# A prefix-conditioned diffusion block on one core: changes at its front, in the work beside the expert blocks, and in how the last two expert blocks reach the output

## The chip, the cores and the metric

The kernel runs on one core of a Trainium2 chip. The metric is the device time of one execution in microseconds (us); the time of the kernel before is the median of three runs. The profile comes from one further, profiled execution.

The engines are named as in the profile: PE (matrix products), PEld (its weight loads), DVE (vector), ACT (scalar functions), POOL (general), SP (only issues transfers). DMA is the core's 16 DMA engines. Each engine works through its own instructions in order and waits on semaphores of the others.

## The reference

512 latent tokens (x) and 256 context tokens (ctx), 1024 wide, all float32, one layer:

```python
sh1, sc1, g1, sh2, sc2, g2 = _modulation(c, w_mod, b_mod, 6)
hx = _rmsnorm(x, norm_mix_pre) * (1 + sc1) + sh1      # the same for ctx
# projections of hx and hc by w_in; a retention scan and a gated
# delta-rule scan, both in two directions, started from the context's state;
# gated merge, output projection
x = x + g1 * _rmsnorm(mixer_out, norm_mix_post)
h2 = _rmsnorm(x, norm_ffn_pre) * (1 + sc2) + sh2
x = x + g2 * _rmsnorm(_moe(h2), norm_ffn_post)
```

In `_moe` each token picks 8 of 64 experts. Each expert computes `(silu(xe @ w_gate) * (xe @ w_up)) @ w_down` (1024 to 256 to 1024) for its tokens in blocks of up to 128; the results, times the token's weight, are summed by token, and a shared expert is added.

## The kernel before

The work is written in stages, and a scheduler of the kernel's framework orders the instructions of each engine. The order below is that of the profiled execution.

- Front (0 to about 62 us). `w_mod` comes in as 16 pieces of 512 KB (tile `wm`, issued on SP at L300) that take turns in five buffers. Each piece is split into a high and a low part (`wmu`: ACT cast L100, DVE difference L107), because a float32 product is made as three products of such parts (L111 to L113). Then x and ctx are normalized (L286) and turned (L338).
- Delta-rule stage (to about 290 us). `w_in` comes in pieces (`raw`, L148), split into `wu`. The scan's triangular systems are built from `E`, `rk`, `br`, stored to DRAM arrays `cd` and `zd` to change their layout, and solved on DVE in 31 steps. `zd` is filled with zeros first (L382, issued on ACT). `bd` receives the turned betas (L527 to L534).
- Retention stage (290 to about 600 us), output projection, second norm and router (to about 700 us). None of it is changed.
- Expert stage (to about 1390 us). There is one block of 128 tokens for each of the 64 experts, and a 65th block for tokens that did not fit into an expert's first block. The token list of a first block (`slots`) comes from sorting; the ranks (L1311 to L1344) and the function `extra` (L1372) find the tokens of the further block. In step e of the loop (L1410) block e is projected (`proj`: 48 products, accumulated in `acc`), block e-1 is turned and projected down (`down`, products `cs<-wd,aT` at L1258), and the weights of later blocks are converted (`wh`, `wl`) and loaded (`w` and `wgu` in six buffers, `wd` in three). `down` scales its result into `y` and a transfer of POOL adds it to the rows of `acc0` or `acc1` in DRAM (L1263).
- Further blocks. A device loop (`For_i`, L1439) handles blocks beyond the 65th; its count `nx` is computed on the chip and is 0 for these inputs. All engines meet at this loop.
- End. `acc1` is loaded (L1456), added to `acc0` (L1458), squared and summed (L1461), normalized (L127 on POOL, L1464), added to x (L1468, or by adding transfers of POOL for two of the four row tiles, L1466) and stored.

## Time and profile before

| | us |
|---|---|
| median of 3 runs | 1429.2 (1427.99 to 1431.35) |
| the profiled execution | 1428.3 |
| its span | 1426.5 |
| PE busy | 1334.9 (94%) |
| DVE busy | 901.3 (63%) |
| ACT busy | 654.1 (46%) |
| POOL busy | 404.4 (28%) |

The span runs from the first to the last instruction of the profile. PE's busy share is a mean over all stages; what a change in a stage is worth depends on what is waited for in that stage. Half a granted clock (PEclk 0.50 for a stretch) means TensorE at 1.2 GHz instead of 2.4 GHz.

### The profile page before, as it was taken

The numbers are of one execution on the slowest core, as the hardware profiler recorded it, in microseconds if no ns is written. First come the engines' busy times: TensorE is split into PE (matmuls) and PEld (weight loads), VectorE is DVE, ScalarE is ACT, GpSimd is POOL, SyncE is SP. The second block draws the span as 40 slices with busy tenths as digits, with TensorE's granted clock in tenths as the row PEclk, the third lists the DMA queues.
The fourth block names the chain that finished last, engine by engine and source line by source line (L and its number), as shares of the span: only waits on it lengthen the run. The fifth ranks groups of instructions, "written<-read, shape, count | busy, mean of one in ns | idle before, by whom it ended". The sixth has DMA issues, their size and how long they took to land.

```text
span 1426.5 us, 20707 instructions
## 1 busy us (share of the span) xinstructions
PE 1334.9 (94%) x7848; PEld 1081.8 (76%) x7848; DVE 901.3 (63%) x1269; ACT 654.1 (46%) x926; POOL 404.4 (28%) x330
## 2 busy tenths in 40 slices
PE   6989888899999999999989999999999999999990
PEld 2658777898887777777878787888888787878770
DVE  5635696457676556547676666666666666666643
ACT  5634431553333222334445555565655555555531
POOL 0313644865320000012402222222222222223312
PEclk9899998999999999999999999999999999999995
DMA  8643521202326578575889999999999999999954
GB/s 291 187 111 104 132 59 27 59 16 80 81 56 181 173 218 233 149 244 198 302 305 339 355 367 342 369 348 354 363 361 358 362 371 350 367 355 360 314 182 126
DMA packets 138841, 340.51 MB, mean 239 GB/s; under 512 B 28218, under 2 KB 84574, under 8 KB 113780
## 3 DMA queue, kind: packets, MB, share of 16 engines
q1 hardware_dynamic: 110952, 289.46, 57.1%
q0 software_dynamic: 19584, 38.99, 10.8%
q10 hardware_dynamic: 8204, 10.72, 2.5%
q8 instruction: 63, 1.03, 0.3%
q14 instruction: 38, 0.31, 0.1%
HBM read 326.59 MB, written 48.31 MB: 263 GB/s over the span
## 4 chain that ended last, share of the span: by engine, by line
PE 46%; DMA 5%; DVE 1%; POOL 1%; issue 0%; ACT 0%; DVEq 0%; SPq 0%; POOLq 0%; ACTq 0%
PE cs L1258 15%; PE acc L112 8%; PE acc L111 8%; PE acc L113 8%; PE ci L1227 4%; DMA wd<-in_w_down_dram 2%; PE ci L1057 2%; DMA wgu<-in_w_up_dram 1%; PE acc L1247 1%; PE acc L1069 1%; DMA w<-acc 1%; POOL fr L127 0%; DMA acc<-y,sl_i 0%; DMA acc<-y,slots 0%; PE ci L1010 0%
## 5 line engine op out<-in xcount | busy, mean ns | idle before, releaser
L111 PE MATMUL acc<-wh,xT 128*128 128x256 f32 x1040 | 305.2, 293 | 0.0
L113 PE MATMUL acc<-wh,xT 128*128 128x256 f32 x1040 | 294.7, 283 | 0.0
L112 PE MATMUL acc<-wl,xT 128*128 128x256 f32 x1040 | 294.4, 283 | 0.0
L1164 DVE TENSOR_TENSOR wl<-w,wh 128x2048 fp32r<-128x2048 f32 x88 | 201.5, 2292 | 87.8 <-PE acc L112 87.7
L1263 POOL DMA_INDIRECT acc<-y,slots x64 | 101.9, 1592 | 479.8 <-ACT y L1260 430.2
L1258 PE MATMUL cs<-wd,aT 128*128 128x512 f32 x520 | 234.3, 593 | 3.3 <-DMA wd<-in_w_down_dram 2.2
L1162 ACT CAST wh<-w 128x2048 fp32r<-128x2048 f32 x88 | 167.2, 1902 | 94.4 <-PE acc L113 76.3
L111 PEld LDWEIGHTS acc<-wh,xT 128*128 128x128 f32 x1040 | 199.9, 192 | 0.2 <-issue 0.2
L112 PEld LDWEIGHTS acc<-wl,xT 128*128 128x128 f32 x1040 | 199.7, 192 | 0.2 <-issue 0.2
L113 PEld LDWEIGHTS acc<-wh,xT 128*128 128x128 f32 x1040 | 199.2, 191 | 0.0
L1258 PEld LDWEIGHTS cs<-wd,aT 128*128 128x128 f32 x520 | 93.9, 190 | 97.3 <-issue 94.7
L1230 DVE TENSOR_TENSOR xT<-ci,xT 128x512 fp32r<-128x512 f32 x130 | 89.3, 687 | 89.7 <-ACT xT L1229 86.2
L100 ACT CAST wu<-raw 128x1024 fp32r<-128x1024 f32 (+1 forms) x73 | 74.9, 1036 | 110.3 <-DMA raw<-in_w_in_dram 76.2
L1164 DVE TENSOR_TENSOR wl<-wgu,wh 128x2048 fp32r<-128x2048 f32 x42 | 96.3, 2292 | 42.7 <-PE acc L112 41.5
L111 PE MATMUL acc<-hTx,wu 128*128 128x512 f32 (+1 forms) x296 | 119.3, 403 | 1.8 <-ACT wu L100 1.8
L113 PE MATMUL acc<-hTx,wu 128*128 128x512 f32 (+1 forms) x296 | 118.3, 400 | 1.6 <-DVE wu L107 1.6
L112 PE MATMUL acc<-hLx,wu 128*128 128x512 f32 (+1 forms) x296 | 117.9, 398 | 0.0
L107 DVE TENSOR_TENSOR wu<-raw,wu 128x1024 fp32r<-128x1024 f32 (+1 forms) x61 | 77.5, 1277 | 62.8 <-ACT wu L100 62.8
L1162 ACT CAST wh<-wgu 128x2048 fp32r<-128x2048 f32 x42 | 79.7, 1898 | 53.8 <-PE acc L113 36.5
L1227 PEld LDWEIGHTS ci<-ident,xg 128*128 128x128 f32 x520 | 73.6, 192 | 29.9 <-issue 29.5
L1219 POOL DMA_INDIRECT xg<-h2d,slots x64 | 71.5, 1117 | 35.6 <-issue 18.3
L1227 PE MATMUL ci<-ident,xg 128*128 128x128 f32 x520 | 80.4, 279 | 0.0
(492 smaller groups left out, 2362.4 us busy)
## 6 DMA issues: line engine op xcount, KB each, us to landing
wd<-in_w_down_dram SPq DMA_DIRECT2D x64, 1024.0 KB
w<-in_w_gate_dram SPq DMA_DIRECT2D x43, 1024.0 KB
w<-in_w_up_dram SPq DMA_DIRECT2D x43, 1024.0 KB
raw<-in_w_in_dram SPq DMA_DIRECT2D x56, 512.0 KB
wgu<-in_w_gate_dram SPq DMA_DIRECT2D x21, 1024.0 KB
wgu<-in_w_up_dram SPq DMA_DIRECT2D x21, 1024.0 KB
mraw<-in_w_mod_dram SPq DMA_DIRECT2D x32, 512.0 KB
wm<-in_w_mod_dram SPq DMA_DIRECT2D x16, 512.0 KB
```

The lines of the kernel that those rows point to most:

```text
L100: nc.scalar.copy(dst, src)
L107: (self.nc.gpsimd if eng == "pool" else self.nc.vector).tensor_tensor(dst, src, hi.bitcast(F32), op=OP.subtract)
L111: mm(out, ah, bh, start=start, stop=False)
L112: mm(out, ah, bl, start=False, stop=False)
L113: mm(out, al, bh, start=False, stop=stop)
L1162: nc.scalar.copy(h[:, i:i + max(n, 1024)], w[:, i:i + max(n, 1024)])
L1164: eng(l[:, i:i + n], w[:, i:i + n], h[:, i:i + n].bitcast(F32), op=OP.subtract)
L1219: nc.gpsimd.indirect_dma_start(xg[:, :], None, self.h2d[:, :], bass.IndirectOffsetOnAxis(ap=ix, axis=0), bounds_check=511, oob_is_err=False)
L1227: nc.tensor.transpose(ps[:, k * 128:k * 128 + 128], xv[:, :, c * 4 + k], self.ident)
L1230: tt(l, ps, h.bitcast(F32), op=OP.subtract)
L1258: nc.tensor.matmul(ps, aT[:, m], wd[:, s], start=k == 0, stop=k == 1)
L1263: nc.gpsimd.indirect_dma_start(self.accd[acc][:, :], bass.IndirectOffsetOnAxis(ap=sx, axis=0), y[:, :], None, bounds_check=511, oob_is_err ...
```

## The change

1. The `wm` pieces 3 to 10 go to eight slices of the storage that later holds `hTx` and `hLx`, so there are eleven buffers instead of five.
2. The zeros for `zd` are written in rows of 774 elements instead of 258, out of `gcv`, and the transfer is issued on ACT behind the copy of `gT`.
3. The turned betas (`bd`) are made behind the first two `prep` calls, and the first q projection ahead of the loop over `vtok`.
4. Ranks, the columns of the further block and its list are made in steps 3, 5 and 7 of the expert loop instead of ahead of it.
5. Blocks 63 and 64 are no longer added to DRAM. Their results are split in two parts (`yhl`, `down_parts`) and a one-hot matrix (`places`) times each part puts the rows in place, in eight PSUM banks; `acc0 + acc1` is added to that. x is loaded for all four row tiles, and all stores are plain ones.
6. The loop over further blocks stands behind the stores, and would do the end again after each block.

```diff
+        wms = [t[:, i] for t in [self.hxpool.tile([128, 4, 1024], F32, name="wm", tag=tag) for tag in ("b0", "b1")] for i in range(4)]
...
-                w = (self.rawp if i % 5 < 3 else wp).tile([128, 1024], F32, name="wm", tag="raw")
+                w = wms[i - 3] if 3 <= i < 11 else self.rawp.tile([128, 1024], F32, name="wm", tag="raw")
...
-        zero = gp.tile([128, 258], F32, name="zero", tag="E")
+        zero = gcv[:, 2:4].rearrange("p a n -> p (a n)")[:, 0:774]
         nc.gpsimd.memset(zero, 0.0)
-        nc.scalar.dma_start(zd.rearrange("t h n -> (t h n)").rearrange("(p a n) -> p a n", p=128, n=258), zero[:, None, :].to_broadcast([128, 12, 258]))
...
-        nc.scalar.copy(gT[:, 0:512], px[0:16])
+        with tc.issue_after(nc.scalar.copy(gT[:, 0:512], px[0:16]).ins):
+            nc.scalar.dma_start(zd.rearrange("t h n -> (t h n)").rearrange("(p a n) -> p a n", p=128, n=774), zero[:, None, :].to_broadcast([128, 4, 774]))
...
-        for t in range(6):
+        prep(0)
+        prep(1)
+        for dr in range(2):
+            ps = self.pc()
+            brd = gc.tile([128, 6, 4], F32, name="brd", bufs=2)
...
+            nc.sync.dma_start(bd[dr], bt)
+        for t in range(2, 6):
             prep(t)
...
+        q0 = conv_in(0, False)
         for t in range(6):
             pk = self.pc()
...
+        def down_parts(aT, ws, wd):
+            y = T8("yhl")
+            for c in range(2):
+                ps = self.pc()
...
+                h, l = y[:, c * 512:c * 512 + 512], y[:, 1024 + c * 512:1536 + c * 512]
+                nc.scalar.activation(h, ps, AF.Copy, scale=ws)
+                nc.vector.scalar_tensor_tensor(l, ps, ws, h.bitcast(F32), op0=OP.mult, op1=OP.subtract)
+            return y
...
+        def places(oh, row):
+            at = q.tile([128, 4], F32, name="at", bufs=2)
+            for t in range(4):
+                ts(at[:, t:t + 1], row, -128.0 * t, None, op0=OP.add)
+                ts(oh[:, t], cst("r0"), at[:, t:t + 1], None, op0=OP.is_equal)
...
+            def place(t, j):
+                oh, y = blocks[j]
+                for c in range(2):
...
+                    for i in range(2):
+                        nc.tensor.matmul(PS[t, c], oh[:, t], y[:, i * 1024 + c * 512:i * 1024 + c * 512 + 512],
+                                         start=j == 0 and i == 0, stop=j == len(blocks) - 1 and i == 1)
+
+            def out(t, s, eng):
+                nc.vector.scalar_tensor_tensor(mg[t][:, s], mg[t][:, s], r[:, t:t + 1], x1[t][:, s], op0=OP.mult, op1=OP.add)
+                eng.dma_start(self.out[t * 128:t * 128 + 128, s], mg[t][:, s])
...
+            for t in range(4):
+                for c in range(2):
+                    s = slice(c * 512, c * 512 + 512)
+                    tt(m[t][:, s], PS[t, c], m[t][:, s], op=OP.add)
...
+                nc.scalar.activation(junk, m[t], AF.Square, scale=D ** -0.5, accum_out=r[:, t:t + 1])
+                nc.scalar.activation(r[:, t:t + 1], r[:, t:t + 1], AF.Identity, bias=self.eps)
+                if t % 2 == 0:
+                    tt(mg[t], m[t], g2p, op=OP.mult)
+                    nc.gpsimd.tensor_tensor(r[:, t:t + 1], r[:, t:t + 1], self.mhalf, op=OP.pow)
+                else:
+                    nc.gpsimd.tensor_tensor(mg[t], m[t], g2p, op=OP.mult)
+                    nc.gpsimd.tensor_tensor(r[:, t:t + 1], r[:, t:t + 1], self.mhalf, op=OP.pow)
+                if t:
+                    out(t - 1, slice(0, 1024), nc.scalar if t % 2 else nc.sync)
+            out(3, slice(0, 512), nc.scalar)
+            out(3, slice(512, 1024), nc.sync)
...
-        self.xtra = extra()
         for e in range(NE + 2):
...
+            if e == 3:
+                ranks()
+            if e == 5:
+                xcols = extra_cols()
+            if e == 7:
+                self.xtra = extra_list(*xcols)
...
-            if e > 0:
-                down(aT, SL[e - 1], W[e - 1], raw(e - 1, 2), 1 if e - 1 > NE - 4 else (e - 1) % 2)
+            if e > NE - 1:
+                Y.append(down_parts(aT, W[e - 1], raw(e - 1, 2)))
+            elif e > 0:
+                down(aT, SL[e - 1], W[e - 1], raw(e - 1, 2), (e - 1) % 2)
...
+            if e == NE - 1:
+                m1, x1 = halves(NE - 2), halves(NE - 1)
...
+            if e == NE:
+                m = halves(NE)
+                for t in range(4):
+                    nc.sync.dma_start(m[t], self.accd[0][t * 128:t * 128 + 128])
+                for t in range(4):
+                    tt(m[t], m[t], m1[t], op=OP.add)
+
+        finish(m, x1, list(zip(OH, Y)))
```

Three places show how the order moves. The first is ACT in the delta-rule stage, where `wu<-raw` converts pieces of `w_in`, `rcA` and `rcB` are copies of products that wait for those, and `gT` is a later one. Before:

```order
L100 CAST wu_620<-raw_618 128x1024
L382 DMA zd_497<-zero_500 1536x1x258
L415 COPY rcA_595<-acc_525 128x512
L415 COPY rcA_597<-acc_526 128x512
L100 CAST wu_637<-raw_635 128x1024
L100 CAST wu_654<-raw_652 128x1024
L100 CAST wu_715<-raw_713 128x128
L415 COPY rcB_669<-acc_599 128x512
L415 COPY rcB_671<-acc_600 128x512
L434 COPY gT_768<-acc_718 16x512
```

Now:

```order
L100 CAST wu_614<-raw_612 128x1024
L417 COPY rcA_589<-acc_519 128x512
L417 COPY rcA_591<-acc_520 128x512
L100 CAST wu_631<-raw_629 128x1024
L100 CAST wu_648<-raw_646 128x1024
L100 CAST wu_709<-raw_707 128x128
L100 CAST wu_820<-raw_818 128x1024
L417 COPY rcB_663<-acc_593 128x512
L417 COPY rcB_665<-acc_594 128x512
L100 CAST wu_885<-raw_883 128x1024
L436 COPY gT_762<-acc_712 16x512
L437 DMA zd_493<-gcv_481 512x1x774
```

The store of the zeros has moved from between the pieces that feed `rcA` and `rcB` to behind `gT`, with a third of the rows.

The second is PE at the start of the expert loop, around the down projection of block 0 (`cs<-wd,aT`); `ci<-colx,oh` are the products of the further block's list, `ci<-ident,xg` turns gathered tokens, `acc<-...,xT` projects a block. Before:

```order
L113 MATMUL acc_5976<-wh_5922,xT_5784 128x256
...
L1258 MATMUL cs_6056<-wd_5609,aT_6009 128x512 x2
L1370 LDWEIGHTS oh_5877
L1370 MATMUL ci_5876<-colx_5866,oh_5877 128x6
L1370 LDWEIGHTS oh_5880
L1370 MATMUL ci_5876<-colx_5866,oh_5880 128x6
L1227 MATMUL ci_5959<-ident_61,xg_5691 128x128
L1370 LDWEIGHTS oh_5883
L1370 MATMUL ci_5876<-colx_5866,oh_5883 128x6
...
L1227 MATMUL ci_5966<-ident_61,xg_5691 128x128 x4
L1227 MATMUL ci_6044<-ident_61,xg_5692 128x128 x4
```

Now:

```order
L1236 MATMUL ci_5864<-ident_61,xg_5686 128x128 x4
L1236 MATMUL ci_5871<-ident_61,xg_5686 128x128 x4
...
L1256 MATMUL acc_5911<-ident_61,sg_5855 128x128 x2
...
L1236 MATMUL ci_5949<-ident_61,xg_5687 128x128 x4
L1267 MATMUL cs_5957<-wd_5604,aT_5914 128x512 x2
L1267 MATMUL cs_5961<-wd_5604,aT_5914 128x512 x2
L1236 MATMUL ci_5969<-ident_61,xg_5687 128x128 x4
```

The products on `colx` are gone from behind the down projection, and the turning of block 2 stands ahead of it.

The third is DVE at the end: `w` and `wgu` are the buffers that hold `acc0`, `acc1` and x there, `fr` the norm's factor. Before:

```order
L1439 COMPARE_AND_BRANCH
...
L1458 TENSOR_TENSOR w_5607<-w_5607,wgu_5604 128x1024 x2
L1458 TENSOR_TENSOR w_5608<-w_5608,wgu_5604 128x1024
...
L126 TENSOR_SCALAR fr_12389<-fr_12389 128x1 x2
L1464 SCALAR_TENSOR_TENSOR w_5607<-w_5607,fr_12389,g2p_5839 128x1024
...
L1464 SCALAR_TENSOR_TENSOR w_5608<-w_5608,fr_12389,g2p_5839 128x1024 x2
L1468 TENSOR_TENSOR w_5608<-w_5608,w_5606 128x1024 x2
```

Now:

```order
L1536 TENSOR_TENSOR w_5602<-w_5602,wgu_5599 128x1024
L1285 SCALAR_TENSOR_TENSOR yhl_12195<-cs_12196,xg_5687,yhl_12195 128x512
...
L1285 SCALAR_TENSOR_TENSOR yhl_12195<-cs_12201,xg_5687,yhl_12195 128x512
L1536 TENSOR_TENSOR w_5603<-w_5603,wgu_5599 128x1024 x2
L1285 SCALAR_TENSOR_TENSOR yhl_12219<-cs_12220,sl_w_6554,yhl_12219 128x512
L1285 SCALAR_TENSOR_TENSOR yhl_12219<-cs_12225,sl_w_6554,yhl_12219 128x512
L1323 TENSOR_TENSOR w_5602<-acc_12233,w_5602 128x512
L1323 TENSOR_TENSOR w_5602<-ci_12236,w_5602 128x512
...
L1330 TENSOR_TENSOR mg_12230<-w_5602,g2p_5800 128x1024
...
L1310 SCALAR_TENSOR_TENSOR mg_12230<-mg_12230,fr_12232,w_5600 128x1024
...
L1310 SCALAR_TENSOR_TENSOR mg_12231<-mg_12231,fr_12232,w_5601 128x512 x2
```

The sums of the two accumulators now stand ahead of and between the low parts of the last two blocks, and the branch of the loop over further blocks is behind all of it.

## Rows read from the trace of the kernel before

**Rows 1.** Windows: stretch, length, busy by engine (instructions), PEclk, DMA share, GB/s.

```profile
0.00:10.00 10.00, 0.37 (x1) 0.18 (x1) 1.44 (x10) 4.45 (x7) 1.35 (x6) 1.00 0.76 241
...
70.00:80.00 10.00, 5.04 (x18) 3.41 (x18) 1.43 (x2) 1.24 (x2) 0.00 (x0) 0.85 0.79 154
...
90.00:100.00 10.00, 8.85 (x54) 5.29 (x53) 2.93 (x11) 3.64 (x8) 0.00 (x0) 1.00 0.01 2
...
180.00:200.00 20.00, 15.70 (x82) 13.46 (x81) 19.31 (x33) 8.05 (x14) 7.57 (x5) 0.83 0.19 53
...
730.00:740.00 10.00, 7.34 (x40) 6.96 (x41) 6.25 (x16) 3.56 (x5) 2.67 (x2) 0.66 0.71 250
...
1200.00:1300.00 100.00, 100.00 (x645) 81.81 (x644) 66.34 (x60) 57.67 (x69) 28.36 (x20) 1.00 1.01 361
...
1340.00:1390.00 50.00, 46.97 (x288) 36.88 (x286) 25.11 (x23) 20.50 (x28) 12.32 (x9) 1.00 0.67 211
```

**Rows 2.** The chain that ended last, from 1300 us: start, length, what.

```profile
1301.14 0.45 PE ci L1227 x4
...
1311.46 0.45 PE ci L1227 x4
...
1325.69 29.83 DMA wd<-in_w_down_dram
...
1389.91 4.64 DMA acc<-y,slots
...
1401.39 8.79 DMA w<-acc
1410.21 1.23 DVE w L1458
1411.58 3.20 POOL fr L127 x3
...
1419.68 1.14 DVEq L1487
```

**Rows 3.** PE's waits, 0 to 300 us: releaser, total, times, longest.

```profile
PE cs L717 <- ACT gcv L501: 4.3, 1, 4.3
...
PE acc L111 <- ACT wmu L100: 2.3, 1, 2.3
PE acc L112 <- DVE wmu L107: 2.1, 3, 1.5
```

**Rows 4.** Timeline of ACT, from 61 us: start, length, instruction.

```profile
63.01 0.58 ACTq L382 DMA_DIRECT2D zd<-zero  x1
```

**Rows 5.** DMA queues, 55 to 90 us (ACT's): packets, MB, share of 16 engines.

```profile
q10 hardware_dynamic: 1552, 1.59, 24.1%
```

**Rows 6.** Timeline of PE, 70 to 84 us.

```profile
70.53 0.40 PE L111 MATMUL acc<-wu,hTc 128*128 128x512 f32 x1
...
73.10 0.40 PE L113 MATMUL acc<-wu,hLc 128*128 128x512 f32 x1
77.99 0.79 PE L111 MATMUL acc<-wu,hTc 128*128 128x512 f32 x1 [4.50 <-ACT wu L100]
...
83.69 0.44 PE L113 MATMUL acc<-wu,hLc 128*128 128x512 f32 x1
```

**Rows 7.** Timeline of PE, 732 to 740 us.

```profile
732.62 0.21 PE L1370 MATMUL ci<-colx,oh 128*128 128x6 bf16 x2 [3.91 <-DVE colx L1356]
...
733.55 3.23 PE L1227 MATMUL ci<-ident,xg 128*128 128x128 f32 x14
736.43 0.56 PE L111 MATMUL acc<-wh,xT 128*128 128x256 f32 x1
...
739.14 0.29 PE L111 MATMUL acc<-wh,xT 128*128 128x256 f32 x1
```

**Rows 8.** Groups by line and shape: count, busy, mean ns, idle before them.

```profile
L1230 DVE TENSOR_TENSOR xT<-ci,xT 128x512 fp32r<-128x512 f32 x130 | 89.3, 687 | 89.7 <-ACT xT L1229 86.2 <-issue 3.4
...
L629 POOL TENSOR_TENSOR bv<-vtok,be 128x512 f32<-128x512 f32 x12 | 13.7, 1141 | 10.8 <-PE cs L641 10.7
```

More of the change, by code (lines that the diff above doesn't have):

```diff
@@ L209, in run @@
         nc.vector.memset(self.mhalf, -0.5)
+        self.eps = main.tile([128, 1], F32, name="eps")
+        nc.vector.memset(self.eps, EPS)
         self.vecT = main.tile([128, 68], F32, name="vecT")
@@ L526, in phaseG @@
             stt(nD[:, l], br[:, :, 0:4], odd[:, l:l + 1], nD[:, l], op0=OP.mult, op1=OP.add)
-        for dr in range(2):
-            ps = self.pc()
-            brd = gc.tile([128, 6, 4], F32, name="brd", bufs=2)
-            nc.vector.tensor_copy(brd, br[:, :, dr * 4:dr * 4 + 4])
-            nc.tensor.transpose(ps[0:24, 0:128], brd.rearrange("p t h -> p (t h)"), self.ident)
-            bt = gc.tile([24, 128], F32, name="bt", bufs=2)
-            nc.scalar.copy(bt, ps[0:24, 0:128])
-            nc.sync.dma_start(bd[dr], bt)
         ZT, QE, CTs = {}, {}, {}
@@ L725, in phaseG @@
         for h in range(4):
[L726 removed]
+            conv(h, qx[:, h], None, q0 if h == 0 else None)
         pq = self.pc()
@@ L1308, in phaseM @@
         r1 = cst("r0")
-        tlt, oneb = p.tile([128, 128], BF, name="tlt"), p.tile([128, 128], BF, name="oneb")
-        ts(tlt, r1, cst("pidx")[:, 0:1], None, op0=OP.is_gt)
-        nc.gpsimd.memset(oneb, 1.0)
-        f = lambda x: x.rearrange("p c e -> p (c e)")
-        ps = self.pi()
-        for t in range(4):
-            if t > 1:
-                nc.tensor.matmul(ps[:, t * 64:t * 64 + 64], oneb, selb[:, t - 2], start=True, stop=False)
-            nc.tensor.matmul(ps[:, t * 64:t * 64 + 64], tlt, selb[:, t], start=t < 2, stop=True)
@@ L1318, in phaseM @@
-        pc = self.pi()
-        for c in (0, 2, 1, 3):
-            nc.tensor.matmul(pc[:, c % 2 * 64:c % 2 * 64 + 64], oneb, selb[:, c], start=c < 2, stop=c > 1)
-        over = p.tile([128, 2, 64], F32, name="over")
-        ts(f(over), pc[:, 0:128], -64.0, 0.0, op0=OP.add, op1=OP.max)
-        for t in range(4):
-            s = slice(t * 64, t * 64 + 64)
-            if t % 2:
-                nc.vector.scalar_tensor_tensor(posm[:, t], ps[:, s], 65.0, over[:, 0], op0=OP.add, op1=OP.add)
-            else:
-                ts(posm[:, t], ps[:, s], 65.0, None, op0=OP.add)
@@ L1400, in extra, with extra_list @@
             fill(colx, wx[:, :, None], 1)
+            return wi, px, colx
+        def extra_list(wi, px, colx):
             ps = self.pi()
@@ L1405, in extra @@
             slot_of(pv, 1, sl)
+            self.xrow = sl[0]
             return wi, sl[1], sl[2]
-        self.xtra = extra()
         x = lambda e: [XT[e][:, h] for h in range(2)]
+        halves = lambda e: [raw(e, n)[:, i * 1024:i * 1024 + 1024] for n in range(2) for i in range(2)]
+        Y = []
         for e in range(NE + 2):
+            if e == NE:
+                OH = T8("oh").rearrange("p (b t n) -> p b t n", b=4, t=4)
+                OH = [OH[:, 0], OH[:, 1]]
+                row = q.tile([128, 1], F32, name="row", bufs=1)
+                nc.vector.tensor_copy(row, slots[:, NE - 1:NE])
+                places(OH[0], row)
+                places(OH[1], self.xrow)
+            if e == 3:
[4 more added lines that the diff above has]
+                self.xtra = extra_list(*xcols)
             if e <= NE:
@@ L1443, in phaseM @@
                 turn(xT, c, xg)
+            to = [raw(NE - 2, 0), raw(NE - 2, 1), raw(NE, 2)]
             for n in range(3):
-                load(NE, n, wi)
-            w = [conv(raw(NE, n), tt, 1024) for n in range(2)]
+                load(NE, n, wi, to[n])
+            w = [conv(to[n], tt, 1024) for n in range(2)]
             pgu = self.pa()
```

120 lines of the change are left out of this document (74 added, 46 removed).

## The prediction

> **What bounds the kernel now.** I read the table of windows first, since the busy shares of the page mix stages. It shows three kinds of stretch [rows 1]. In the expert loop (1200 to 1300 us) PE is busy without a gap while the DMA engines are full as well, share 1.01 at 361 GB/s. Around 180 to 200 us DVE is the full one (19.31 of 20 us) and PE has gaps. In a few short stretches nothing is full: 70 to 80 us (PE 5.04 of 10), 730 to 740 us (PE 7.34, and the clock at 0.66) and the end. Then the chain that ended last [rows 2]: in the loop it steps from PE to PE, and the turning of one half block at 1301.14 comes again at 1311.46, so a block takes 10.32 us. At the end it is a series of single steps: an adding transfer, the load of acc1 (8.79 us), sums on DVE, POOL and DVE steps in turn. The waits and timelines of the short stretches give the terms below. All of them are made against the profiled execution, 1428.3 us, of which the span is 1426.5; it is 0.9 below the median, 1429.2, and I add that at the end.
>
> **The front loads.** In the first ten microseconds the DMA engines are busy 0.76 [rows 1], because the pieces of w_mod wait for five buffers. With eleven, SP issues on. PE waits 2.3 us for conversions (ACT) and 2.1 us for the low parts (DVE) there [rows 3]. The first depends on arrival, the second on DVE's own speed. I take -2.0, between 0 (the last pieces still wait for a buffer, and x stands behind them on SP) and -4.4 (both waits). x_0 goes ahead of the last two pieces; its share of the load time is paid by them, so nothing for it.
>
> **The zeros of zd.** The store is issued at 63.01 us on ACT [rows 4], beside the pieces of w_in. In the 35 us from 55 on, ACT's queue takes 24.1% of the engines for 1.59 MB [rows 5], 8.4 us of all sixteen. PE pays for it: twelve products on one piece take from 70.53 to 73.10 plus one pitch of 0.23, 2.8 us; the next twelve run from 73.33, wait 4.50 us for the conversion, and go on at the half clock to about 83.9 [rows 6]. That is 10.6 us for 2.8 us of work, 7.8 lost. Now the store stands behind gT, 10 us or more later, where the DMA share is 0.01 (90 to 100 us) [rows 1], and its rows are three times as long. What queues behind it on ACT is the second half of the gT copy, which it doesn't delay. I take -7.5. At least 4.5 goes, the wait alone, if the clock falls all the same; at most 8. Everything after it, the chain on DVE included, starts earlier by as much.
>
> **Betas and q ahead.** The wait of 4.3 us at L717 [rows 3] is what moving q0 fills, but it lies in the stretch in which DVE is busy 19.31 of 20 us and PE is not what is waited for [rows 1]. So PE's gap closes and opens again further on. The moves also put POOL's low parts of a w_in piece and SP's load of it ahead of stores that the DVE chain needs. I take +0.5, and half the 4.3 either way as bounds, -2 to +2.5. The constant eps costs one small memset beside loads, nothing.
>
> **Ranks and lists in the loop.** Before, PE stands 3.91 us behind the down projection of block 0, waiting for colx from DVE [rows 7]. That goes. The clock fell there: 14 turns take from 733.55 to 736.43, 0.206 us each, against 0.45/4 = 0.112 in the loop [rows 2, 7]; sixteen cost 1.5 us more than they need. The first twelve products of block 2 take from 736.43 to 739.14, 2.71 us, and half of that at the full clock, 1.35 more. Together 6.8. What is late next: the rank products stood in a stretch where PE was dense and still do; the four products on colx, some 0.25 us, now come at e = 7. DVE gets some 10 us of small operations spread over five blocks, with a third of each block free (66.34 of 100 us busy) [rows 1]. SP's read of nx moves six loads further down the stream, still behind the ranks on DVE by a block or less, while the load behind it waits for a buffer of the same step. I take -6.5; between -4 (the wait alone, to the nearest) and -8.
>
> **The end.** Before, the adding transfer of block 63 starts at 1389.91 and the span ends at 1426.5, 36.6 us. After, on the same clock: the load of acc0 waits for the adding transfer of block 62, one block before that of 63: 1389.91 - 10.32 + 4.64 = 1384.2. Four loads take 8.79 as those of acc1 did [rows 2], so the last lands near 1394. DVE, in order, has four sums of 1.23 us (L1458) and four low parts of about 0.7 between them; the low parts stand behind the first sums, and PE's placement of block 63, and behind it the down projection of 64, wait for them. The sums of tile 3 and the low parts of block 64 end near 1397, the first placement near 1397.5. Then DVE has eight adds out of the PSUM banks (0.69 each, as L1230 [rows 8]), two products and four final operations (1.23 to 1.28 each): 5.5 + 2.5 + 5 = 13, so 1410.5, and about 2.5 for the last square, product and power behind the last add. The last store is issued near 1413, against 1419.68 + 1.14 = 1420.8 [rows 2]. From there to the end I take the same 5.7 us and 1.3 for the loop's meeting of all engines, which stood ahead of the loads and now stands behind the stores. 1420.0 instead of 1426.5: -6.5. If the loads land as soon as the engines have room (share 0.67 from 1340 on [rows 1]), DVE starts some 4 us earlier: -11. If POOL and DVE hold each other up, as below, -2.
>
> The low end of that comes from a row. Three powers on 128x1 take POOL 3.20 us while DVE adds two operands from SBUF [rows 2], and DVE's add beside them is not longer than others (1.23). So it is POOL that was held up. The Trainium skill (SBUF — State Buffer, "Who interferes with whom") says that a DVE instruction with two SBUF inputs and a POOL instruction that reads SBUF exclude each other for a whole instruction, and that the one that starts first wins. The row agrees in one direction. By the rule POOL's two products of 128x1024 would hold DVE up as well.
>
> **Sum.** -2.0 - 7.5 + 0.5 - 6.5 - 6.5 = -22.0. 1428.3 - 22.0 + 0.9 = 1407.2; I say 1407.
>
> **The rivals.**
>
> First: the transfers bound the expert loop, and what PE gains at its start is waited for later. For it: share 1.01 at 361 GB/s from 1200 to 1300, and a weight that takes 29.83 us to land at 1325 [rows 1, 2], so the cushion of loaded weights is used up by the end. Against it: PE has no gap in those 100 us, and the share is only 0.71 from 730 to 740, 2.9 us of room that the change fills. Price: the 6.5 of the loop's start. 1413.7. The Trainium skill (DMA: Bandwidth & Descriptors, "Specifications") puts the limit of HBM for one core at about 358 GB/s. The window's 361 GB/s agrees with such a limit, and a stream at it can't catch up.
>
> Second: the end is held up by POOL. The two products of 128x1024 take about 2 x 1.14 us each [rows 8]; if DVE stands still during both, 4.6 us go back. 1411.8. For it: the row of the powers. Against it: half of DVE's operations there read PSUM.
>
> Third: the zeros are not the cause, and the pieces of w_in land late by themselves. Price 7.5: 1414.7. Against it: 8.4 us of the engines in just that stretch [rows 5].
>
> Fourth, the other side: at the end the loads of acc0 stand in SP's queue behind the last weight, x and acc1. If they wait as that weight did, 29.83 us, and then take 8.79, the last lands at 1384.2 + 29.8 + 8.8 = 1422.8 instead of 1394, and DVE, the placements and the stores wait for it: +29, 1436. It decides against the change from a landing of 1419 on. Against it: the share has fallen to 0.67 from 1340 on [rows 1], so that the queue has run empty by then.
>
> **How the numbers follow.** The forecast 0.56, the first rival 0.18, the second 0.13, the third 0.06, the fourth 0.05; 0.02 for several misses that cancel the gain. No change means within 0.2%, 2.9 us, about what a measurement of this kernel can tell. All but the last two are faster: 0.93, the same 0.02, slower 0.05. The range: the lower ends of the terms sum to -4.4 - 8 - 2 - 8 - 11 = -33.4, the upper ones to 0 - 4.5 + 2.5 - 4 - 2 = -8. All terms will not fall on one end, so 1397 to 1421, which takes in the first three rivals and leaves out the fourth.
>
> **What would show it.** The zeros: in the window of 70 to 80 us PE near 10 at clock 1.00, and no wait for wu beyond 1 us. The loop's start: no wait for colx, PE full between blocks 0 and 2 with the clock at 1.00, and steps of 10.32 after it; waits for wd or wgu late in the loop are the first rival's. The end: last adds near 1410 and the last store near 1413 on before's clock; long DVE steps beside POOL's products are the second rival's, a wait of DVE for w or wgu beyond a few microseconds the fourth's. The forecast is wrong as a whole if the loop's pace is no longer 10.3 us a block.

## The result: 16 us faster, and where they came from

The changed kernel takes 1412.9 us in the median of six runs (1410.5 to 1417.0), the kernel before, run beside it, 1429.3 (1427.5 to 1431.4). The ratio is 0.989, with a 95% interval of 0.987 to 0.991. The forecast was 1407, the range 1397 to 1421. The profiled execution's span is 1412.2 us against 1426.5. That is 14.3 less and not 16.3, because the profiled run of after lies 1.2 above its median and that of before 0.9 below.

One operation found in both traces at each stage's border tells where the 14.3 us come from. The last column is what each stage adds.

| start of | before | after | difference | stage |
|---|---|---|---|---|
| last ACT cast of `hTc` (front) | 54.70 | 55.90 | +1.2 | +1.2 |
| ACT copy of `gT` (behind the pieces of w_in) | 94.13 | 86.32 | -7.8 | -9.0 |
| down projection of block 0 | 725.01 | 717.92 | -7.1 | +0.7 |
| down projection of block 1 | 744.15 | 728.24 | -15.9 | -8.8 |
| down projection of block 63 | 1385.32 | 1369.59 | -15.7 | +0.2 |
| end of the span | 1426.5 | 1412.2 | -14.3 | +1.4 |

The front gave nothing, the zeros 9.0, the start of the expert loop 8.8, and the new end took 1.4 more than the old one instead of 6.5 less. The windows of after, beside those of before [rows 1], show the first two of these gains: PE is nearly full at the full clock in 70 to 80 us and in 730 to 740, where it was at 5.04 and 7.34 of 10.

```profile
70.00:80.00 10.00, 9.42 (x54) 7.78 (x53) 4.86 (x6) 4.52 (x6) 3.95 (x4) 1.00 0.75 194
...
180.00:200.00 20.00, 17.12 (x80) 13.75 (x79) 19.47 (x25) 8.83 (x16) 9.01 (x6) 0.91 0.19 53
730.00:740.00 10.00, 10.00 (x76) 8.48 (x75) 9.12 (x25) 5.29 (x9) 2.72 (x2) 1.00 0.99 354
1200.00:1300.00 100.00, 99.78 (x634) 80.29 (x633) 65.41 (x59) 57.02 (x68) 27.84 (x18) 1.00 1.00 353
1340.00:1390.00 50.00, 43.36 (x228) 31.74 (x227) 25.96 (x35) 15.49 (x23) 5.71 (x4) 0.93 0.57 188
```

The last window, 43.36 of 50 us against 46.97 [rows 1], can't be compared by the clock on the wall: after is 15.7 us ahead there, and the same stretch counted from block 63, 1355.7 to 1405.7 us in before, has PE busy for 37.14 at clock 0.92. What is new at the end stands in PE's waits of after from 600 us on (in all, times, longest). The wait for `colx` is gone, and a wait of 6.6 us for the low part of a block has come. The waits for `wd` are those of before (2.2 us, two times).

```profile
PE acc L1306 <- DVE yhl L1285: 6.6, 1, 6.6
PE cs L1267 <- DMA wd<-in_w_down_dram: 2.3, 2, 1.9
```

The chain that ended last in after, from 1298 us (start, length, what), answers to [rows 2].

```profile
1298.16 29.76 DMA wd<-in_w_down_dram
...
1328.06 5.37 PE cs L1267 x8
...
1363.82 0.70 ACT y L1269
...
1364.78 9.93 DMA acc<-y,slots
1374.76 3.48 DMA w<-acc
...
1380.28 1.22 PE acc L1306 x2
...
1381.93 4.57 PE cs L1282 x8
...
1391.70 3.31 POOL mg L1333
...
1402.54 0.55 POOL fr L1334
1403.12 0.56 DVE mg L1310
```

The adding transfer of block 62, for which the loads of `acc0` wait, takes 9.93 us, not the 4.64 of [rows 2]. Behind it come the loads, the sums, a down projection of block 64 of 4.57 us where the same eight products take 3.43 to 3.45 (the granted clock is 0.50 from 1378 to 1384 us, behind the wait of 6.6), and two products of POOL that DVE waits for. DVE's timeline of after shows the same stations: the first sum of the accumulators after a wait of 7.71 us for `acc`, the first add out of PSUM, and two final operations that wait for POOL.

```profile
1378.34 1.23 DVE L1536 TENSOR_TENSOR w<-w,wgu 128x1024 f32<-128x1024 f32 x1 [7.71 <-DMA w<-acc]
1379.48 0.74 DVE L1285 SCALAR_TENSOR_TENSOR yhl<-cs,xg,yhl 128x512 fp32r<-128x512 f32 x1
...
1387.91 0.69 DVE L1323 TENSOR_TENSOR w<-acc,w 128x512 f32<-128x512 f32 x1
...
1395.56 1.30 DVE L1310 SCALAR_TENSOR_TENSOR mg<-mg,fr,w 128x1024 f32<-128x1024 f32 x1 [1.55 <-POOL fr L1334]
...
1403.12 1.41 DVE L1310 SCALAR_TENSOR_TENSOR mg<-mg,fr,w 128x512 f32<-128x512 f32 x2 [2.74 <-POOL fr L1334]
```

### The profile page after: what moved, and what is told of

The parts are those of the page before. It is cut to its first block, busy times and chain, and to the rows that moved or that the text cites. A ratio compares the mean times of both kernels' runs of the same rounds, so it can differ in the third digit from the quotient of the medians.

```text
span 1412.2 us, 20821 instructions
## 1 busy us (share of the span) xinstructions
PE 1333.0 (94%) x7880; PEld 1080.6 (77%) x7880; DVE 912.7 (65%) x1294; ACT 656.5 (46%) x932; POOL 411.5 (29%) x328
## 3 DMA queue, kind: packets, MB, share of 16 engines
q1 hardware_dynamic: 111672, 291.82, 58.1%
## 4 chain that ended last, share of the span: by engine, by line
PE 48%; DMA 3%; DVE 1%; POOL 1%; issue 0%; ACT 0%; POOLq 0%; DVEq 0%; SPq 0%
PE cs L1267 15%; PE acc L113 8%; PE acc L111 8%; PE acc L112 8%; PE ci L1236 4%; DMA wd<-in_w_down_dram 2%; PE ci L1066 2%; PE acc L1256 1%; PE acc L1078 1%; DMA acc<-y,slots 1%; POOL mg L1333 0%; PE cs L1282 0%; DMA w<-acc 0%; DVE w L1323 0%; DVE mg L1310 0%
## 5 line engine op out<-in xcount | busy, mean ns | idle before, releaser
L1267 PE MATMUL cs<-wd,aT 128*128 128x512 f32 x504 | 228.7, 597 | 2.6 <-DMA wd<-in_w_down_dram 2.3
L111 PEld LDWEIGHTS acc<-wh,xT 128*128 128x128 f32 x1040 | 196.7, 189 | 0.2 <-issue 0.2
L112 PEld LDWEIGHTS acc<-wl,xT 128*128 128x128 f32 x1040 | 196.2, 189 | 0.2 <-issue 0.2
L113 PEld LDWEIGHTS acc<-wh,xT 128*128 128x128 f32 x1040 | 195.8, 188 | 0.0
L100 ACT CAST wu<-raw 128x1024 fp32r<-128x1024 f32 (+1 forms) x73 | 75.1, 1036 | 105.9 <-DMA raw<-in_w_in_dram 68.1
L1228 POOL DMA_INDIRECT xg<-h2d,slots x64 | 76.4, 1194 | 35.6 <-issue 17.7
```

The source lines that it names most:

```text
L100: nc.scalar.copy(dst, src)
L111: mm(out, ah, bh, start=start, stop=False)
L112: mm(out, ah, bl, start=False, stop=False)
L113: mm(out, al, bh, start=False, stop=stop)
L1228: nc.gpsimd.indirect_dma_start(xg[:, :], None, self.h2d[:, :], bass.IndirectOffsetOnAxis(ap=ix, axis=0), bounds_check=511, oob_is_err=False)
L1267: nc.tensor.matmul(ps, aT[:, m], wd[:, s], start=k == 0, stop=k == 1)
```

## The experiments

Each is the changed kernel with one part undone or altered, timed beside the kernel before; all ratios are to it, and 0.0007 of the ratio is 1 us. "Tail" is the time from the down projection of block 63 to the span's end: 41.2 us before, 42.6 after. How far the front has come when `hTc` is done differs between kernels by some microseconds (53.3 to 58.1), so within a trace I count from there. The kernel after itself was timed in one comparison only, ahead of these. Three kernels that undo only edits found to be worth little measured 0.9895 to 0.9909, so its ratio may well be nearer the upper end of its interval, 0.9905, and a difference from 0.989 below 0.0015 says nothing.

**Zeros at the old place, in the old rows.**

```diff
+        zero = gp.tile([128, 258], F32, name="zero", tag="E")
+        nc.gpsimd.memset(zero, 0.0)
+        nc.scalar.dma_start(zd..., zero[:, None, :].to_broadcast([128, 12, 258]))
-        with tc.issue_after(nc.scalar.copy(gT[:, 0:512], px[0:16]).ins):
-            nc.scalar.dma_start(zd..., zero[:, None, :].to_broadcast([128, 4, 774]))
+        nc.scalar.copy(gT[:, 0:512], px[0:16])
```

> The changed kernel, but with the zeros of zd stored in rows of 258 at the old place, beside the pieces of w_in. Theory: this one store costs the 7.8 us by which gT came earlier; 1420.7, with the wait of about 10 us for raw on ACT back and PE near 5 of 10 us in 70 to 80. Rival: the pieces land late by themselves and the eleven buffers at the front made the difference: within 1 us of 1412.9.

Measured: 0.9975 (0.9964 to 0.9986), 1422.4 us. PE's timeline has the wait of before [rows 6] again, at the same piece, and ACT, which converts that piece, waits 10.36 us for it to land (10.32 in before, 3.71 in after). PE is busy for 4.62 of the 10 us from 70 to 80.

```profile
76.32 0.56 PE L111 MATMUL acc<-wu,hTc 128*128 128x512 f32 x1 [4.68 <-ACT wu L100]
77.58 0.80 PE L112 MATMUL acc<-wu,hTc 128*128 128x512 f32 x1 [0.70 <-DVE wu L107]
...
75.22 1.24 ACT L100 CAST wu<-raw 128x1024 fp32r<-128x1024 f32 x2 [10.36 <-DMA raw<-in_w_in_dram]
```

`gT` starts 39.4 us after the last `hTc` (53.31 to 92.67), as in before (54.70 to 94.13), against 30.4 in after (55.90 to 86.32). So the store costs 9.0 us in the trace; by the times it is 8.6 thousandths, 12 us, or 10 if after is at 0.9905. The third rival, that the pieces of w_in land late by themselves, falls.

**Zeros issued ahead, in the long rows.** This was to tell the place of the store from the length of its rows.

```diff
         nc.gpsimd.memset(zero, 0.0)
+        nc.scalar.dma_start(zd..., zero[:, None, :].to_broadcast([128, 4, 774]))
...
-        with tc.issue_after(nc.scalar.copy(gT[:, 0:512], px[0:16]).ins):
-            nc.scalar.dma_start(zd..., zero[:, None, :].to_broadcast([128, 4, 774]))
+        nc.scalar.copy(gT[:, 0:512], px[0:16])
```

> The kernel after with the store of the zeros issued at its old place on ACT (behind the memset, ahead of the conversions of w_in), but in the new rows of 774 elements. Tells the place of the store from the length of its rows. With 258-element rows at the old place the copy of gT came 7.8 us later and the ratio was .9975. Theory: it is the bytes that collide with the pieces of w_in, so longer rows give little back: 5 to 8 us lost, gT near 92 us, ratio .993 to .997. Rival: it is the count of short rows that costs; then the long rows lose under 3 us, gT near 88, ratio .988 to .990.

Measured: 0.9952 (0.9936 to 0.9967), in the theory's range, but not for its reason. The view of this tile (duration in ns, first and last start) shows the issue at 33.2 us, not near 62: the new source, `gcv`, is free early, while the old one shared its storage with `E`.

```profile
L385 ACTq DMA_DIRECT2D zd<-gcv x1: 601/601/601, 33.2 to 33.2; - x1
```

There the store meets the loads of x and not the pieces of w_in behind `hTc`: `hTc` is done at 58.09, the latest of all kernels, and `gT` starts 33.0 us after it. So the store costs something there too, presumably beside the loads of x, and the length of the rows was not separated from the place. It stays open what share the longer rows have.

**Ranks and lists ahead of the loop again.**

```diff
         Y = []
+        ranks()
+        self.xtra = extra_list(*extra_cols())
         for e in range(NE + 2):
-            if e == 3:
-                ranks()
...
```

> The changed kernel, but with ranks, columns and list of the further block made ahead of the expert loop. Theory: PE's wait and the half clock at the start of the loop come back and stay to the end, since the loop is paced by PE: 8.7 us, 1421.6. Rival: the loop's transfers are the bound and swallow the start: 1413 to 1415, with fewer waits for wd near the end of the loop.

Measured: 0.9962 (0.9949 to 0.9975), 1420.7 us. The wait of before is back (PE's waits from 600 us), and the step from block 0 to block 1 is 17.62 us instead of 10.32 (PE's timeline).

```profile
PE ci L1447 <- DVE colx L1433: 3.9, 1, 3.9
...
715.93 3.59 PE L1267 MATMUL cs<-wd,aT 128*128 128x512 f32 x8
...
733.55 3.60 PE L1267 MATMUL cs<-wd,aT 128*128 128x512 f32 x8
```

In return two steps are shorter. In after, the steps in which the ranks and the list are now made (from block 1 to 2 and from 5 to 6) take 10.64 and 10.66 us; here all are 10.27 or 10.28. So the move is worth 7.3 us at the start of the loop in these traces, less 0.8 later: 6.5. The profiled run, 1415.5, is the fastest of its six, so its span of 1413.6 shows less of the loss than the median does. In the trace the loss doesn't vanish into waits for transfers: PE waits 1.7 us for `wd` late in the loop, against 2.3 in after and 2.2 in before.

**Five buffers at the front again.**

```diff
-                w = wms[i - 3] if 3 <= i < 11 else self.rawp.tile([128, 1024], F32, name="wm", tag="raw")
+                w = (self.rawp if i % 5 < 3 else wp).tile([128, 1024], F32, name="wm", tag="raw")
```

> The kernel after with only the first edit undone: the pieces of w_mod take turns in five buffers again. Theory: the additional buffers gain nothing, because the arrival of the pieces and the conversions set the pace; the transposed normalized tokens are complete at the same time as in the other kernels of this call within 1 us, and the time is that of the kernel after within 1 us (ratio to before .987 to .990). Rival (the prediction's first term): 2 us are lost, ratio .990 to .9915, and the low digits of PE's waits for wmu grow by as much.

Measured: 0.9905 (0.9890 to 0.9920), inside the rival's numbers, with PE's waits for `wmu` at 7.1 us in all against 4.9 in after; but `hTc` is done at 56.44, between the others of the same comparison (54.18 to 58.09), as the theory has it. The intervals overlap: whether the buffers are worth 0 or 2 us is not settled by these runs.

```profile
PE acc L111 <- ACT wmu L100: 4.4, 2, 2.4
...
PE acc L112 <- DVE wmu L107: 2.7, 3, 1.4
```

**The q projection back behind the loop over `vtok`.**

```diff
-        q0 = conv_in(0, False)
...
-            conv(h, qx[:, h], None, q0 if h == 0 else None)
+            conv(h, qx[:, h], None)
```

> The kernel after with only the early q projection undone (it stands behind the loop over vtok again). Theory: in the stretch of the 31 steps DVE is what is waited for, so PE's gap only changes its place: the time is that of the kernel after within 1 us, and a wait of some 4 us of PE for gcv comes back at the first q projection. Rival: the early projection saves what PE's wait was, 2.5 to 4 us, ratio .990 to .992.

Measured: 0.9895 (0.9881 to 0.9909), no difference. The wait for `gcv` is 5.0 us again, where after has 2.7, and nothing came of it. The theory holds.

```profile
PE cs L725 <- ACT gcv L508: 5.0, 1, 5.0
```

**The turned betas back ahead of the `prep` calls.** The q projection stays where after has it.

```diff
+        for dr in range(2):
+            ... (the turned betas)
...
-        prep(0)
-        prep(1)
-        for dr in range(2):
-            ... (the turned betas)
-        for t in range(2, 6):
+        for t in range(6):
             prep(t)
```

> The changed kernel, but with the betas' transposes and stores ahead of prep(0) as before (the early q projection stays). Theory: their move let POOL take two low parts of a w_in piece (3.5 us) ahead of the last two QE products, so the last CT and with it the chain on DVE lost about 2.7 of the 9.4 us gained upstream; undone, the last CT comes near 157.6 instead of 160.25 and the time is about 1410.2. Rival: the loss is from the early q projection or from DVE itself, the time stays at 1412.9 (+-1).

Measured: 0.9909 (0.9894 to 0.9923), 1413.7 us, which is the rival's number and not the theory's 1410.2. The theory's mechanism is there all the same: SP's load of the systems, `M<-cd`, stands 74.6 us behind `gT` (84.81 to 159.44) instead of 77.0 (86.32 to 163.33), because in after POOL makes two low parts of w_in and a memset ahead of the last two factors `QE`. POOL's timeline of after:

```profile
152.21 3.52 POOL L107 TENSOR_TENSOR wu<-raw,wu 128x512 fp32r<-128x512 f32 x2 [2.15 <-ACT wu L100]
156.41 1.81 POOL L563 MEMSET W<- 96x2048 f32 x1 [0.67 <-DVE QE L546]
158.18 2.04 POOL L548 TENSOR_TENSOR QE<-QE,rk 128x512 f32<-128x512 f32 x2
```

But by the start of the expert loop they are lost again, and more: from `gT` to the down projection of block 0 it is 636.6 us, against 631.6. Most of this is PE's clock, in the output projection, which no edit touches: from 638 to 644 us it is 0.50 here and 1.00 in after (first row here, second after), and from the first write to `mix` to the start of its last it is 44.9 us against 41.5.

```profile
638.00:644.00 6.00, 6.00 (x22) 5.23 (x22) 4.00 (x16) 2.30 (x4) 2.35 (x2) 0.50 0.53 180
...
638.00:644.00 6.00, 6.00 (x35) 5.27 (x36) 5.33 (x16) 2.94 (x5) 2.35 (x3) 1.00 0.62 221
```

The traces of two further kernels below, with all products on DVE, have the same fall, and the other eleven don't have it there. Each of the three profiled executions is the longest of its kernel (a single one of 7532 us aside), so the fall may well belong to the execution and not to the edit. What sets it off was not found, nor what the betas are worth by themselves.

**The end of before, with all other edits.** `acc1` takes blocks 61 to 64 by adding transfers, and the loop over further blocks stands ahead of the loads.

```diff
-            if e > NE - 1:
-                Y.append(down_parts(aT, W[e - 1], raw(e - 1, 2)))
-            elif e > 0:
-                down(aT, SL[e - 1], W[e - 1], raw(e - 1, 2), (e - 1) % 2)
+            if e > 0:
+                down(aT, SL[e - 1], W[e - 1], raw(e - 1, 2), 1 if e - 1 > NE - 4 else (e - 1) % 2)
...
-        finish(m, x1, list(zip(OH, Y)))
```

> The changed kernel, but with the end as before: all blocks added to DRAM, the loop over further blocks ahead of the last loads. Theory (from the trace of the changed kernel, where the stretch from the down projection of block 63 to the end is 42.5 us against 41.0 before): 1411.5, the new end is not shorter. Rival (the forecast): the old end is 6.5 us longer, 1419.4.

Measured: 0.9879 (0.9863 to 0.9895), 1407.8 us; the tail is 41.0 us against 42.6. The old end is as good as the new one or better, though the ratio says more than the tail: the loop runs at 10.20 us a block here instead of 10.27, some 3.5 us over its length. The chain shows what an adding transfer takes when nothing is loaded beside it:

```profile
1366.75 4.67 DMA acc<-y,slots
1372.25 4.66 DMA acc<-y,sl_i
1378.22 8.79 DMA w<-acc
```

**The sums behind the low parts.** The four sums of the accumulators wait for the last low part of block 64.

```diff
-                for t in range(4):
-                    tt(m[t], m[t], m1[t], op=OP.add)
...
+        with tc.issue_after(self.low.ins):
+            for t in range(4):
+                tt(m[t], m[t], m1[t], op=OP.add)
         finish(m, x1, list(zip(OH, Y)))
```

> The changed kernel, but with the four sums acc0 + acc1 behind the low parts of blocks 63 and 64 on DVE. Theory: DVE's wait for acc0 (7.7 us) holds the low part of block 63, which PE waits 6.6 us for, and behind it the down projection of block 64; with the low parts first PE has no wait above 1.5 us, the first add out of PSUM comes 4.6 us earlier against the down projection of block 63, and the stretch from that projection to the end is 37.9 instead of 42.5 us; 1408.3. Rival: the arrival of acc0 is the bound and DVE only trades one wait for another; stretch 42 or more, 1412 to 1413.

Measured: 0.9877 (0.9861 to 0.9892), 1410.0 us; tail 38.3 us, near the theory's 37.9. PE has no wait left there, block 64 is projected at 1374.87 in 3.63 us, and the first add out of PSUM comes 14.3 us after the down projection of block 63 (1370.16 to 1384.46), against 18.3 in after. DVE's timeline, low part, sums, first add:

```profile
1379.26 0.75 DVE L1285 SCALAR_TENSOR_TENSOR yhl<-cs,sl_w,yhl 128x512 fp32r<-128x512 f32 x1 [0.97 <-ACT yhl L1284]
1379.92 4.62 DVE L1538 TENSOR_TENSOR w<-w,wgu 128x1024 f32<-128x1024 f32 x4
1384.46 0.68 DVE L1323 TENSOR_TENSOR w<-acc,w 128x512 f32<-128x512 f32 x1
```

**All products by `g2p` on DVE.**

```diff
-                if t % 2 == 0:
...
-                    nc.gpsimd.tensor_tensor(mg[t], m[t], g2p, op=OP.mult)
...
+                tt(mg[t], m[t], g2p, op=OP.mult)
```

> The changed kernel, but with all four products by g2p on DVE (POOL keeps the powers). Theory: POOL's product of 128x1024 takes 3.31 us because DVE's operations on two operands from SBUF hold it up, and DVE then waits 1.55 and 2.74 us for the power behind it; on DVE it takes 1.22. The stretch from the down projection of block 63 to the end is 2 us shorter, 40.5; 1410.9. Rival: the two engines share the work at no loss, and DVE gets 2.4 us more: 44.9, 1415.3.

Measured: tail 40.9 us, as expected; the ratio, 0.9905 (0.9890 to 0.9920), does not show it (one run of 7532 us, unexplained, is left out of it). In its trace the down projection of block 0 starts at 724.86, 6.9 us later than in after, long before the products come; PE's clock is 0.50 from 642 to 648 us there, and the writes to `mix` take 45.9 us. DVE's waits for the norm's factor fall from 4.3 to 0.4 us, for two more products of 1.2.

**Block 62 placed too, and the sums behind a low part.** `acc0` is loaded first and `acc1` last, so that the loads no longer wait for the transfer of block 62.

```diff
-            if e > NE - 1:
+            if e > NE - 2:
                 Y.append(down_parts(aT, W[e - 1], raw(e - 1, 2)))
...
-                    nc.sync.dma_start(m1[t], self.accd[1][t * 128:t * 128 + 128])
+                    nc.sync.dma_start(m1[t], self.accd[0][t * 128:t * 128 + 128])
...
-                    nc.sync.dma_start(m[t], self.accd[0][t * 128:t * 128 + 128])
+                    nc.sync.dma_start(m[t], self.accd[1][t * 128:t * 128 + 128])
```

> The changed kernel, but with block 62 placed by one-hot products as well (three blocks), acc1 as the later of the two loads, and the sums behind the low part of block 63. Theory: the adding transfer of block 62 took 9.9 us beside the loads of acc1 and x, against 4.6 before, and held the load of acc0; without it the last load lands near 1370, the sums are done near 1376 and the adds start when PE has placed the first tile, near 1381.5: stretch from the down projection of block 63 to the end 36, 1406.5. Rival: sixteen more products and a third pair of parts on PE, ACT and DVE take what is won: 41 to 43, 1412 to 1413.

Measured: 0.9881 (0.9866 to 0.9896); tail 35.3 us, near the theory's 36 and 3.0 shorter than in the run before the last, where only the order was turned. DVE has no wait for the loads left, and POOL's two products stand in the chain again (3.38 and 1.97 us of it).

**Both: block 62 placed, and all products on DVE.** The two diffs above together.

> The kernel after with block 62 placed by one-hot products too (so that acc1 holds blocks 1 to 61 and its loads come last, with acc0 loaded first), the sums of the accumulators behind the low parts of block 63, and all four products by g2p on DVE. Theory: the end of the kernel after is paid for in three separate places, the adding transfer beside the loads (9.93 us instead of 4.64), the sums ahead of the low parts, and POOL's two products that DVE waits for (1.55 + 2.74 us). The first two are already gone with block 62 placed (35.3 us from the down projection of block 63 to the span's end, 42.6 in the kernel after); taking POOL's products away brings it to 33.5 to 34.5, because DVE then does two products of 1.27 more and waits 4.3 less. Ratio to the kernel before .982 to .987. Rival: the stretch is set by PE's placements, and the products on DVE only add 2.5 us: 37 to 38 us, ratio .989.

Measured: 0.9865 (0.9849 to 0.9881), 1408.5 us; tail 33.2 us. By the ratio it is the fastest of these that does all the work, 19.0 below before; its interval still touches that of after. DVE's timeline is nearly closed (sums, first add, last operations):

```profile
1380.14 4.62 DVE L1535 TENSOR_TENSOR w<-w,wgu 128x1024 f32<-128x1024 f32 x4
...
1386.01 0.69 DVE L1323 TENSOR_TENSOR w<-acc,w 128x512 f32<-128x512 f32 x1
...
1399.87 1.42 DVE L1310 SCALAR_TENSOR_TENSOR mg<-mg,fr,w 128x512 f32<-128x512 f32 x2 [0.44 <-POOL fr L1330]
```

Its tail is 9.4 us shorter than that of after, and the time only 3 to 6 (from 0.9889 or 0.9905). The rest is lost ahead of the loop, 6.3 us between `gT` and the down projection of block 0: the clock's fall in the output projection (45.1 us for the writes to `mix` against 41.5), and a wait of PE for gathered tokens, which after doesn't have:

```profile
PE ci L1236 <- DMA xg<-h2d,slots: 3.0, 1, 3.0
```

**Without the loop over further blocks.** This leaves out the blocks beyond the 65th, of which there are none for these inputs.

```diff
-        cnt = nc.values_load(nx[0:1, 0:1], min_val=0, max_val=62)
-        with tc.For_i(0, cnt) as _:
-            wi, ix, ws = extra_list(*extra_cols())
...
```

> The changed kernel without the loop over further blocks, which runs 0 times for these inputs (blocks beyond the 65th would be left out). Theory: the meeting of all engines behind the stores costs what the end after the last store is longer than before, 7.6 - 5.7 = 1.9 us: 1411.0. Rival: the time after the last store is the landing of that store, and the loop is hidden behind it: 1412.9.

Measured: 0.9865 (0.9850 to 0.9880), 1409.2 us; tail 38.2 us, 4.4 less than after and more than twice what the theory gave. SP's row of the last stores ends at 1406.08, and the span at 1408.7, 2.6 us on:

```profile
1398.02 8.06 SPq L1311 DMA_DIRECT2D out_dram<-mg  x2
```

In after the same row ends at 1404.93 and the span at 1412.2, 7.3 us on.

```profile
1396.88 8.05 SPq L1311 DMA_DIRECT2D out_dram<-mg  x2
```

## Why the prediction was right in sum and wrong at the end

The time fell by 16.3 us where 22.0 were forecast. The sign is right, the three terms that carry it are not all right. By the table, four of the five terms lie outside their own bounds: the zeros and the lists gained more than their best, the front and the end less than their worst. That the sum lies well inside the range is in part luck, for the errors have both signs.

- **The front loads, forecast -2.0: between 0 and -2 by the run with five buffers, +1.2 in the trace, open.** The share of the DMA engines in the first ten microseconds, which I had put down to the five buffers, is 0.77 with eleven against 0.76: four pieces are issued by 8.1 us in both kernels, and from 4 to 10 us the engines are full in both (0.98 to 1.06 in windows of 2 us), so nothing waited for a buffer there. PE waits 4.9 us for `wmu` in all, against 4.4 [rows 3]. The poorer bound came true as it was described: the last two pieces of w_mod still wait for a buffer, and three of four loads of x stand behind them. SP issues ten pieces by 22 us, but x at 33.27, where before it went at 30.70. SP's timeline of after:

```profile
11.89 10.35 SPq L301 DMA_DIRECT2D wm<-in_w_mod_dram  x10
22.80 0.33 SPq L260 DMA_DIRECT2D x<-in_x_dram  x1
31.65 1.57 SPq L301 DMA_DIRECT2D wm<-in_w_mod_dram  x2
33.27 1.37 SPq L260 DMA_DIRECT2D x<-in_x_dram  x3
```

- **The zeros, forecast -7.5: 9.0 in the trace.** Right in place and mechanism, and undoing it brought back the wait and the time. The bound of 8 was too tight; where the last microsecond went in before I did not find.
- **Betas and q, forecast +0.5: +0.7.** Undoing either by itself changed nothing that the times show; both together were not undone. The price named, POOL's low parts of w_in ahead of the chain, is the one that the trace shows.
- **Ranks and lists, forecast -6.5: -8.8 at the start of the loop.** Right in mechanism; the size depends on how one counts. The step from the down projection of block 0 to that of block 1 was 19.14 us, against 10.32 for a block [rows 2], and is 10.32 now. Of the gain 0.8 goes back in the two longer steps, where I had counted 0.25. And with the lists back the step was 17.62 and not 19.14: PE's clock was at 0.50 for 3.4 us there and for 6.8 in before, by windows of 1 us, with nearly the same wait ahead of it (3.86 and 3.91). By that run the move is worth 6.5, the forecast; by before's trace 8.0. PE's timeline of before:

```profile
725.01 3.70 PE L1258 MATMUL cs<-wd,aT 128*128 128x512 f32 x8 [0.26 <-ACT aT L1249]
...
744.15 3.60 PE L1258 MATMUL cs<-wd,aT 128*128 128x512 f32 x8
```

- **The end, forecast -6.5: +1.4. This is the step that failed.** On before's clock (15.7 us later), the adding transfer of block 62 ends at 1390.4, where I had 1384.2; the first add out of PSUM starts at 1403.6 against 1397.5; the last store is issued by 1420.7 against 1413; and 7.3 us follow instead of 7.0. So the chain was 6.1 late at the first add, lost 1.5 more up to the last store, and 0.3 behind it: 7.9 us, the whole of the miss. The 0.3 is luck: without the loop 2.6 us follow the last store, so that the 5.7 I took for the store and the 1.3 for the loop were both wrong, with opposite signs.
  - The first is the 4.64 us that I took for the adding transfer. That row [rows 2] was the transfer of a block at the very end, with empty queues. In after the transfer of block 62 (1364.78) stands beside four loads of 512 KB of `acc1`, whose issue begins at 1364.31, and takes 9.93. Another 0.9 is that the step from block 62 to 63 takes 9.41 us (1360.18 to 1369.59) and not a whole block's 10.32. The loads behind it gave some back: the DMA engines are done with them at about 1381.4, 6.7 us behind the transfer and not 8.79. The trace of before had the long case too, two transfers ahead of the one I used: POOL's transfer of 1371.22, beside four loads of an accumulator and two of x whose issue begins at 1370.09, for which the next one waited until 1381.95, 10.7 us on. In all ten traces with the new end and two placed blocks the loads of `acc0` are issued 9.5 to 10.5 us behind this transfer. That the loads lengthen it was read from these cases and not tried by itself. Placing block 62 as well, so that nothing waits for this transfer, takes the tail to 35.3, but that run turns the order on DVE as well, which alone gives 38.3: the two were not tried apart.

```profile
1371.22 1.58 POOL L1263 DMA_INDIRECT acc<-y,slots  x1 [0.30 <-issue]
1381.95 1.56 POOL L1263 DMA_INDIRECT acc<-y,slots  x1 [9.14 <-DMA acc<-y,slots]
```

  - Once the loads are late, the order on DVE, sums ahead of low parts, makes them late for PE as well. I had named that wait and let it cost nothing, since all sums and low parts had to be done anyway. But PE's clock falls in those 6.6 us, and its placements and the projection of block 64 come after the sums instead of beside them. Turning the order round, with the transfer still at 9.7 us, brings the first add 4.0 us nearer to the down projection of block 63 (14.3 against 18.3), most of the 6.1, and is worth 4.3 us of tail. So with the loads as late as they were, most of the loss came through this order.
  - The second rival was right in part. POOL's product takes 3.31 us, not 1.14 for half the size [rows 8], and DVE waits 4.3 us in all for its results. DVE's own operations beside it are not longer (1.27 to 1.30). The exclusion that the Trainium skill describes (SBUF — State Buffer, "Who interferes with whom") fits POOL's side: in every trace the product starts 0.16 or 0.17 us behind an operation of DVE on two operands from SBUF that has 1.1 us to run, and by an estimate from the rows 1.1 plus twice 1.14 is 3.4. But there is no instance without such an operation to compare with, so this is not shown. DVE's side is not tested here: beside POOL's product it has only that operation, which had started first, and adds out of PSUM.
- **The rivals.** The first, transfers that bound the loop, did not come. After waits 2.3 us for `wd` in two places, with the clock lower behind the longer one (5.37 us for a projection of 3.44), but before waits 2.2 in two places too. The last seven steps up to block 63 are 1.6 us longer in after than in before (75.1 against 73.6), yet in the ten other kernels that keep the lists in the loop and some form of the new end they take 73.3 to 74.4, so this is mostly the one execution. What spoke for the rival, 361 GB/s as a ceiling, falls as well: the trace of before reaches 394 GB/s from 30 to 40 us, and that of after 401 from 20 to 30. An unforeseen pace of 10.27 instead of 10.32 us a block, less the two longer steps, had gained 1.4 up to there, so that nothing is left of either. The third fell. The fourth did not come: the first of the loads landed 3.5 us after its issue.

Against the forecast of -22.0 the spans moved -14.3. The end misses 7.9, the front 3.2 (which its variation alone can make), the betas and the loop's pace 0.2 each; the zeros and the lists give 1.5 and 2.3 back.

## What to carry to other kernels

Take a transfer's duration from an instance that has the same neighbours in the queues as it will have, not from the cleanest one: here 4.64 and 10 us stood a few rows apart. Where a stall lowers PE's clock, subtract whole periods (19.14 - 10.32) as a check on the pieces that one can name, and take off what the moved work costs where it lands (0.8 here). An order written for DVE should put first what another engine waits for, even where DVE has to do all of it anyway.

## What the runs showed of the hardware

- A loop that is run zero times costs 4.4 us when it stands behind the last stores (tail 42.6 with it, 38.2 without); I had taken 1.3 for its meeting of all engines. Which part of it the engines' meeting takes was not separated.
- The expert loop, whose code is not changed in these steps, takes 10.32 us a block in before, 10.27 in after and in the other kernels made from it, and 10.20 in the one with the old end. The projection's products differ by as much: 282 and 283 ns in the rows of before over 860 to 1060 us, 281 and 282 in after, 279 and 280 with the old end. What sets it was not found. The groups with the old end:

```profile
L113 PE MATMUL acc<-wh,xT 128*128 128x256 f32 x312 | 87.3, 280 | 0.0
L112 PE MATMUL acc<-wl,xT 128*128 128x256 f32 x312 | 87.2, 279 | 0.0
```

- A POOL product of 128x1024 takes 3.31 to 3.38 us in ten traces, each time starting while DVE works on two operands from SBUF.
- PE's granted clock fell to 0.50 for some 7 us of the output projection in three of fourteen traces, and the writes to `mix` took 44.9 to 45.9 us there, in the others 40.7 to 42.3. A wait of PE of 1.67 us for `h` stands ahead of it, in after as well, where the clock stays at 1.00.
